# Projection weights kept in DRAM as split halves between two super-blocks

## Chip, core and metric

The kernel runs on one core of a Trainium2 chip. The metric is the device time of one execution in microseconds (us). TensorE is called PE below (its weight loads PEld), VectorE DVE, ScalarE ACT, GpSimd POOL. SP is SyncE, which issues all DMAs of this kernel and runs no arithmetic.

## What is computed

With DEPTH = 1 only layer 0 of the reference runs: a gated DeltaNet layer over 2048 tokens of width 1024, with 8 heads of 128, in float32, and a final norm.

```python
h = x + gated_deltanet_mixer(rms_norm(x, a_norm_w), a_w_in, ...)
out = rms_norm(h, final_norm_w)
# the mixer
proj = h @ w_in                                   # 2048x1024 @ 1024x4112
qkv, z, b_raw, a_raw = split(proj)
q, k, v = split(silu(causal_depthwise_conv(qkv, conv_w)))
o = chunk_gated_delta_rule(l2(q), l2(k), v, beta, g_log)   # state S_t, chunk by chunk
y = rms_norm(o, o_norm_w) * silu(z)
return y @ w_out
```

## The kernel before

**Super-blocks and units.** The 2048 tokens are worked in two super-blocks (`sb` 0 and 1) of 1024. A unit is one head in one super-block, so there are 16 units (`u` 0 to 15; the first 8 belong to super-block 0). Before each super-block `phase0` norms eight tiles of x (128 tokens each), transposes them on PE, and keeps them as two float32r halves `xh` and `xl`; `gates` works out the decays and writes them to DRAM as `gd`, from where `decay` reads them broadcast into the tile E and into qe.

**Projections.** A unit needs four weight tiles of 1024 rows by 128 columns: k, q, v and z (`KI`, `QI`, `VI`, `ZI`). `load_w` reads one into the staging tile `wraw` (eight pieces of 512 bytes on each of 128 partitions), and `split_w` makes two halves of it: ACT rounds it to float32r (`hi`), DVE subtracts that from the raw tile (`lo`). `proj` then makes each product of 512 tokens from 24 matmuls: hi with xh, hi with xl, lo with xh, for eight blocks of rows. A pair of halves is used for two blocks of 512 tokens, that is 48 matmuls. The weights do not depend on the super-block, so each of the 32 tiles is loaded and split twice, once in either super-block.

**Buffers.** `hi` and `lo` (and the halves of y in the output stage) live in six buffers that the profile calls `rnd`; `wraw` lives with x tiles, E, U, A and others in eight buffers called `big`; the smaller tiles are in `half`, and PSUM is `bank`.

**The rest of a unit.** `k_side` forms k·k and q·k products and the tile U, `invert` inverts the triangular matrices (U goes to DRAM and back through `d1`, four small writes and one read, the tile called `d` in the profile), `recur` carries the state S over eight chunks: for each chunk PE, DVE and ACT hand work to each other (rho on DVE, n on ACT, S on DVE), with projections of the next unit in between on PE. After all units the output stage multiplies by `w_out`, adds x, norms and writes.

**Order.** Nothing is issued as written: every operation is recorded by the class `Plan` with a due time `prio` (units of one head; `AT` holds the offsets), and `Plan.schedule` lays them out on the five engines by a list scheduler with a cost for each operation and DMA, and with buffers bound as they come free. The resulting order is fixed, each engine runs its own in order, and all instructions have the line of the issue loop, L357. SP, too, works in order: a DMA that waits for its data holds back the DMAs planned behind it. The due time of a weight load is that of its projection plus `AT["w"]` = -0.14, once the due time is 1 or later.

Of the kernel before, what the change touches and what calls it, by code (L numbers as in the profile page):

```python
# [13 lines left out]
F32 = mybir.dt.float32  # L14
# [8 lines left out]
P = 128  # L23
T = 2048
D = 1024
H = 8
# [9 lines left out]
AT = dict(kq0=-0.25, kq1=-0.09, decay=0.0, k0=0.0, k1=-0.07, inv=-0.36, v=0.0, z=-0.58, vside=-0.67, phase=-0.5,  # L36
          gates=-0.31, w=-0.14)
# [324 lines left out]
def tile_gated_deltanet(ctx: ExitStack, tc: tile.TileContext, x, a_norm_w, w_in, conv_w,  # L362
# [5 lines left out]
    dp = ctx.enter_context(tc.tile_pool(name="dp", bufs=1, space=DRAM))  # L368
# [8 lines left out]
    nc = Plan(tc, cp, pp, bufs, shared)  # L377
# [10 lines left out]
    def st(shape, dtype, tag):  # L388
        return nc.tile(tag, shape, dtype)

    def ps(tag, shape=(P, TB)):
        a = nc.tile(tag, (P, TB), F32, psum=True)[0:shape[0], 0:int(np.prod(shape[1:]))]
        return a.rearrange("p (c k) -> p c k", k=shape[2]) if len(shape) > 2 else a
# [125 lines left out]
    def split_w(raw, hi, lo):  # L519
        nc.scalar.copy(hi, raw)  # L520
        nc.vector.tensor_tensor(out=lo, in0=raw, in1=hi.bitcast(F32), op=ALU.subtract)
# [92 lines left out]

    KI, QI, VI, ZI = 1, 0, 2, 3

    def load_w(ty, h):
        hi = st([P, KT, P], F32R, "whi")
        lo = st([P, KT, P], F32R, "wlo")
        raw = st([P, KT, P], F32, "wraw")  # L620
        c0 = ty * D + h * P
        at = nc.prio
        if at >= 1:
            nc.prio = at + AT["w"]
        nc.sync.dma_start(raw, w_in[:, c0:c0 + P].rearrange("(k p) c -> p k c", p=P))
        split_w(raw, hi, lo)
        nc.prio = at
        return hi, lo

    def proj(w, xh, xl, pj, toks=slice(0, TB)):  # L630
        hi, lo = w
        for k in range(KT):
            nc.tensor.matmul(pj[:, toks], lhsT=hi[:, k, :], rhs=xh[:, k, toks], start=(k == 0), stop=False)
            nc.tensor.matmul(pj[:, toks], lhsT=hi[:, k, :], rhs=xl[:, k, toks], start=False, stop=False)
            nc.tensor.matmul(pj[:, toks], lhsT=lo[:, k, :], rhs=xh[:, k, toks], start=False, stop=(k == KT - 1))

    def conv_block(un, ty, tb, pj):
        h = un["h"]
        raw = st([P, CW - 1 + TB], F32, "raw")
        nc.scalar.copy(raw[:, CW - 1:], pj)  # L640
        nc.gpsimd.tensor_copy(raw[:, 0:CW - 1], halo[:, ty * 8 + h, :])
        if tb < NTB - 1 or un["sb"] < NSB - 1:
            nc.gpsimd.tensor_copy(halo[:, ty * 8 + h, :], raw[:, TB:])
        d = half_tile(un, "qkv"[ty], tb)
        nc.scalar.mul(d, raw[:, 0:TB], cwcol(0, ty, h))
        for tap in range(1, CW):
            nc.vector.scalar_tensor_tensor(out=d, in0=raw[:, tap:tap + TB], scalar=cwcol(tap, ty, h), in1=d,
                                           op0=ALU.mult, op1=ALU.add)
        nc.scalar.activation(d, d, AF.Silu)
# [4 lines left out]
    def half_tile(un, tag, j):  # L654
        a = un[tag, j] = st([P, TB], F32, tag)
        return a
# [7 lines left out]
    def project(un, steps, parts=1):  # L664
        for ty, _ in steps:
            if ty not in un["w"]:
                un["w"][ty] = load_w(ty, un["h"])
        pjs = [ps("pj") for _ in steps]
        for i in range(parts):
            for (ty, tb), pj in zip(steps, pjs):  # L670
                proj(un["w"][ty], un["xh"][tb], un["xl"][tb], pj, slice(i * TB // parts, (i + 1) * TB // parts))
                if i < parts - 1:
                    continue
                if ty == ZI:
                    nc.scalar.activation(half_tile(un, "z", tb), pj, AF.Silu)
                else:
                    conv_block(un, ty, tb, pj)
# [248 lines left out]
    NU = NSB * H  # L926
    nc.prio = -0.97
    w_first = {KI: load_w(KI, 0)}
    nc.prio = -0.94
    w_first[QI] = load_w(QI, 0)  # L930
    nc.prio = -0.9
    xhs, xls, pba = phase0(0)
# [4 lines left out]
    for u in range(NU):  # L937
        un = dict(i=u, sb=u // H, h=u % H, xh=xhs, xl=xls, g=gt, w=w_first if u == 0 else {})
        last = u % H == H - 1
        nc.prio = float(u)  # L940
        if prev is not None:
            recur(prev)
        nc.prio = u + AT["kq0"] if u else -0.72
        project(un, ((KI, 0), (QI, 0)), 2 if u == 0 else 1)
        nc.prio = u + AT["decay"]
        decay(un)
        nc.prio = u + AT["k0"]
        k_side(un, 0)
        nc.prio = u + AT["kq1"]
        project(un, ((KI, 1), (QI, 1)))  # L950
        nc.prio = u + AT["k1"]
        k_side(un, 1)
        nc.prio = u + AT["inv"]
        invert(un)
        if last:
            nc.prio = u + AT["v"]
            project(un, ((VI, 0), (ZI, 0), (VI, 1), (ZI, 1)))
        else:
            nc.prio = u + AT["v"]
            project(un, ((VI, 0), (VI, 1)))  # L960
            nc.prio = u + AT["z"]
            project(un, ((ZI, 0), (ZI, 1)))
# [56 lines left out]
```

## Time and profile before

| what | value |
|---|---|
| median of 3 runs | 1241.1 us (1240.69 to 1241.73) |
| the profiled execution's own time | 1240.98 us |
| its span, first to last instruction | 1239.2 us |
| mean granted PE clock | 0.999 |
| busy: PE, PEld, DVE, ACT, POOL | 99%, 83%, 78%, 49%, 14% |
| DMA moved, mean rate | 118.28 MB, 95 GB/s |

The profile is of one execution. Its span leaves 1.8 us of the execution's time outside. Busy shares are means over the whole span; a busy PE is counted from modelled ends of pipelined matmuls, so the distance from one matmul's start to the next one's is the better measure of its pace. A timeline row gives start, duration, engine, line, operation, what it writes and reads, and how often it is repeated; idle time ahead of it and what ended that stand in brackets.

### The profile page before, as it was taken

How to read it: one execution, taken by the hardware profiler on the slowest of the kernel's cores; microseconds unless marked ns; L12 is line 12 of the kernel's file. 1: busy time of each engine (PE TensorE's matmuls, PEld its weight loads, DVE VectorE, ACT ScalarE, POOL GpSimd, SP SyncE). 2: the span in 40 equal slices, each digit the busy share in tenths (PEclk: the TensorE clock that was granted, in tenths of full speed). 3: DMA queues.
4: the chain of work that ended last, by engine and by line, in shares of the span. 5: the costliest groups of instructions: out<-in, count | busy, mean ns of one | idle time of the engine just before them, and what ended most of it. 6: DMA issues, size and time to landing. Idle time of an engine off the chain costs nothing.

```text
span 1239.2 us, 21069 instructions
## 1 busy us (share of the span) xinstructions
PE 1225.3 (99%) x8049; PEld 1024.5 (83%) x8049; DVE 962.2 (78%) x2228; ACT 607.5 (49%) x1297; POOL 170.5 (14%) x265
## 2 busy tenths in 40 slices
PE   8999999999999999999999999999999999999997
PEld 6788888888888888888888888888888888788886
DVE  6779877877787889797878787878787898955553
ACT  5665455544554565557454545463635564322121
POOL 2011011201111312221010202010101020100100
PEclk9999999999999999999999999999999999999999
DMA  7050423232324131422312122222223225547631
GB/s 229 21 165 1 111 66 81 61 81 60 82 61 117 44 96 46 130 71 79 90 54 84 56 81 61 81 61 81 61 82 111 81 86 179 188 128 248 230 102 68
DMA packets 127481, 118.28 MB, mean 95 GB/s; under 512 B 23986, under 2 KB 106515, under 8 KB 127380
## 3 DMA queue, kind: packets, MB, share of 16 engines
q1 hardware_dynamic: 127380, 116.93, 31.5%
q8 instruction: 63, 1.03, 0.4%
q14 instruction: 38, 0.31, 0.1%
HBM read 97.84 MB, written 19.07 MB: 94 GB/s over the span
## 4 chain that ended last, share of the span: by engine, by line
PE 98%; ACT 1%; DVE 1%; issue 0%; DMA 0%; POOLq 0%; POOL 0%; DVEq 0%; ACTq 0%
PE bank L357 98%; ACT half L357 0%; DVE big L357 0%; ACT rnd L357 0%; DVE half L357 0%; DMA big<-in_a_norm_w_dram 0%; ACT L357 0%; DVE rnd L357 0%; ACT xh L357 0%; ACT big L357 0%; DVE xl L357 0%; POOLq L1015 0%; POOL rs L357 0%; ACT raw L357 0%; DVEq L1015 0%
## 5 line engine op out<-in xcount | busy, mean ns | idle before, releaser
L357 PE MATMUL bank<-xh,rnd 128*128 128x512 f32 (+1 forms) x2624 | 871.8, 402 | 0.7 <-ACT xh L357 0.7
L357 PEld LDWEIGHTS bank<-xh,rnd 128*128 128x128 f32 x2624 | 483.0, 189 | 87.9 <-ACT xh L357 1.3
L357 PE MATMUL bank<-xl,rnd 128*128 128x512 f32 (+1 forms) x1328 | 532.5, 401 | 0.1
L357 PEld LDWEIGHTS bank<-xl,rnd 128*128 128x128 f32 x1328 | 251.3, 189 | 43.2 <-DVE xl L357 0.4
L357 DVE SCALAR_TENSOR_TENSOR half<-raw,vcol,half 128x512 f32<-128x512 f32 x288 | 213.5, 747 | 31.4 <-ACT half L357 27.0
L357 DVE TENSOR_TENSOR rnd<-big,rnd 128x1024 fp32r<-128x1024 f32 x80 | 97.7, 1221 | 47.8 <-ACT rnd L357 42.4
L357 ACT CAST rnd<-big 128x1024 fp32r<-128x1024 f32 x80 | 83.8, 1048 | 99.4 <-PE bank L357 86.3
L357 ACT ACTIVATE n<-bank,nb 128x128 f32<-128x128 f32 x128 | 47.4, 370 | 168.4 <-PE bank L357 168.4
L357 ACT ACTIVATE half<-half 128x512 f32<-128x512 f32 x128 | 80.9, 632 | 93.1 <-DVE half L357 92.1
L357 ACT COPY raw<-bank 128x512 f32<-128x512 f32 x96 | 56.2, 585 | 83.6 <-PE bank L357 83.1
L357 DVE TENSOR_TENSOR half<-X,big 128x6 f32<-128x6 f32 (+15 forms) x256 | 93.7, 366 | 4.4
L357 DVE TENSOR_REDUCE X<-half 128x2 f32<-128x6 f32 (+15 forms) x256 | 92.0, 360 | 4.1
L357 POOL COPY halo<-raw 128x3 f32<-128x3 f32 x72 | 23.4, 325 | 481.7 <-ACT raw L357 473.6
L357 ACT ACTIVATE half<-big 128x512 bf16<-128x512 f32 (+1 forms) x48 | 37.1, 773 | 85.4 <-issue 42.9
L357 ACT ACTIVATE half<-raw,vcol 128x512 f32<-128x512 f32 x96 | 69.4, 724 | 5.0 <-DVE vcol L357 1.4
L357 POOL TENSOR_TENSOR sk<-ssk,phalf 128x4 f32<-128x4 f32 x32 | 40.3, 1261 | 171.6 <-DVE ssk L357 169.8
L357 DVE SCALAR_TENSOR_TENSOR rho<-bank,eg,half 128x128 f32<-128x128 f32 x120 | 41.6, 347 | 27.3 <-PE bank L357 26.9
L357 DVE SCALAR_TENSOR_TENSOR S<-S,dend,bank 128x128 f32<-128x128 f32 x112 | 38.6, 345 | 26.0 <-PE bank L357 25.0
L357 POOL TENSOR_TENSOR rs<-ss,nhalf 128x1 f32<-128x1 f32 x32 | 23.6, 737 | 252.3 <-DVE ss L357 245.0
L357 DVE TENSOR_TENSOR big<-bank,big 128x512 f32<-128x512 f32 x32 | 22.1, 691 | 45.2 <-PE bank L357 45.2
L357 ACT ACT_TABLE_LOAD x42 | 53.9, 1283 | 1.5 <-PEq L1003 0.7
L357 PEld LDWEIGHTS bank<-rho,V 128*128 128x128 f32 x256 | 46.8, 189 | 9.2
(116 smaller groups left out, 1615.1 us busy)
## 6 DMA issues: line engine op xcount, KB each, us to landing
big<-in_a_w_in_dram SPq DMA_DIRECT2D x64, 512.0 KB
big<-in_x_dram SPq DMA_DIRECT2D x32, 512.0 KB
big<-gd SPq DMA_DIRECT2D x16, 512.0 KB
half<-gd SPq DMA_DIRECT2D x32, 256.0 KB
big<-d SPq DMA_DIRECT2D x16, 512.0 KB
yd<-half SPq DMA_DIRECT2D x32, 256.0 KB
big<-yd SPq DMA_DIRECT2D x16, 512.0 KB
big<-rd SPq DMA_DIRECT2D x16, 512.0 KB
```

The lines of the kernel that those rows point to most:

```text
L357: ins = getattr(getattr(self.tc.nc, op[6]), op[7])(*args, **kwargs)
```

## The change

`load_w` gets the super-block as an argument. In super-block 0 it does what it did, and then writes both halves to a DRAM tile `w_d`, two DMAs of 512 KB, with 4 KB in one piece for each partition. In super-block 1 it has no `wraw` and no split: two DMAs read the halves from `w_d` straight into the two buffers that the matmuls use. All DMAs go through SP's queue.

```diff
+    w_d = [dp.tile([H, 2, P, D], F32, name=f"wd{t}") for t in range(4)]
+
-    def load_w(ty, h):
+    def load_w(ty, h, sb=0):
         hi = st([P, KT, P], F32R, "whi")
         lo = st([P, KT, P], F32R, "wlo")
+        if sb:
+            at = nc.prio
+            nc.prio = at + AT["w"]
+            nc.sync.dma_start(hi.bitcast(F32).rearrange("p k c -> p (k c)"), w_d[ty][h, 0])
+            nc.sync.dma_start(lo.bitcast(F32).rearrange("p k c -> p (k c)"), w_d[ty][h, 1])
+            nc.prio = at
+            return hi, lo
         raw = st([P, KT, P], F32, "wraw")
...
         nc.sync.dma_start(raw, w_in[:, c0:c0 + P].rearrange("(k p) c -> p k c", p=P))
         split_w(raw, hi, lo)
+
+        nc.sync.dma_start(w_d[ty][h, 0], hi.bitcast(F32).rearrange("p k c -> p (k c)"))
+        nc.sync.dma_start(w_d[ty][h, 1], lo.bitcast(F32).rearrange("p k c -> p (k c)"))
         nc.prio = at
...
-                un["w"][ty] = load_w(ty, un["h"])
+                un["w"][ty] = load_w(ty, un["h"], un["sb"])
```

## Rows read from the trace of the kernel before

**Rows 1.** The page, busy time: us, share of the span, instructions.

```profile
PE 1225.3 (99%) x8049; PEld 1024.5 (83%) x8049; DVE 962.2 (78%) x2228; ACT 607.5 (49%) x1297; POOL 170.5 (14%) x265
```

**Rows 2.** Stretches: length, busy us (instructions) by engine, clock, DMA share, GB/s.

```profile
core 0: us, PE busy (x) PEld busy (x) DVE busy (x) ACT busy (x) POOL busy (x), PEclk, DMA share, GB/s
0.00:36.00 36.00, 30.15 (x180) 25.56 (x181) 24.37 (x45) 20.69 (x38) 9.39 (x25) 1.00 0.70 212
...
36.00:574.00 538.00, 537.76 (x3649) 449.26 (x3648) 438.29 (x1051) 294.97 (x619) 88.01 (x134) 1.00 0.27 75
583.00:1053.00 470.00, 469.77 (x3243) 395.50 (x3244) 385.85 (x916) 239.44 (x529) 54.01 (x86) 1.00 0.28 82
...
1200.00:1240.00 40.00, 31.86 (x140) 25.86 (x138) 13.99 (x29) 4.86 (x14) 2.20 (x4) 0.95 0.22 79
```

**Rows 3.** The chain that ended last, in order of time: start, length, what.

```profile
36.56 537.79 PE bank L357 x3640
574.37 1.05 ACT rnd L357
...
577.49 1.22 DVE rnd L357
...
583.23 648.65 PE bank L357 x4173
1231.90 0.70 DVE big L357
```

**Rows 4.** Timeline of PE, after a change of kind, and at the boundary.

```profile
66.46 0.48 PE L357 MATMUL bank<-xh,rnd 128*128 128x512 f32 x1
66.78 0.39 PE L357 MATMUL bank<-xl,rnd 128*128 128x512 f32 x1
67.02 0.63 PE L357 MATMUL bank<-xh,rnd 128*128 128x512 f32 x2
67.48 0.39 PE L357 MATMUL bank<-xl,rnd 128*128 128x512 f32 x1
...
583.23 0.49 PE L357 MATMUL bank<-half,half 128*128 128x128 f32 x2 [0.43 <-ACT half L357]
```

**Rows 5.** Groups by operation: busy us, mean ns, idle before and its releasers.

```profile
L357 DVE TENSOR_TENSOR rnd<-big,rnd 128x1024 fp32r<-128x1024 f32 x80 | 97.7, 1221 | 47.8 <-ACT rnd L357 42.4 <-PE bank L357 2.7 <-issue 2.4
L357 ACT CAST rnd<-big 128x1024 fp32r<-128x1024 f32 x80 | 83.8, 1048 | 99.4 <-PE bank L357 86.3 <-DVE big L357 12.1 <-DMA big<-in_a_w_in_dram 0.8
...
L357 PE MATMUL bank<-rho,V 128*128 128x128 f32 x256 | 49.1, 273 | 0.0
```

**Rows 6.** Stretches around one raw load, one write, and one write with a read.

```profile
30.40:34.50 4.10, 4.10 (x24) 3.42 (x23) 3.16 (x5) 2.33 (x6) 0.73 (x2) 1.00 0.48 130
1224.90:1228.00 3.10, 3.10 (x15) 2.59 (x14) 0.74 (x3) 0.72 (x2) 0.00 (x0) 1.00 0.42 169
...
1214.00:1219.00 5.00, 5.00 (x23) 4.13 (x22) 1.48 (x4) 0.72 (x2) 0.00 (x0) 1.00 0.60 210
```

**Rows 7.** Timeline of PE: a buffer's last matmul, and the next weight's first.

```profile
546.84 0.39 PE L357 MATMUL bank<-xl,rnd 128*128 128x512 f32 x1
...
553.52 0.40 PE L357 MATMUL bank<-xh,rnd 128*128 128x512 f32 x1
```

**Rows 8.** Timeline, end of super-block 0: a split on DVE, its first matmuls.

```profile
480.25 1.20 DVE L357 TENSOR_TENSOR rnd<-big,rnd 128x1024 fp32r<-128x1024 f32 x1
...
481.80 0.86 PE L357 MATMUL bank<-xh,rnd 128*128 128x512 f32 x3
```

**Rows 9.** Timeline, start: the last first-phase x tile issued by SP, read by ACT.

```profile
18.66 0.33 SPq L357 DMA_DIRECT2D big<-in_x_dram  x1
...
31.49 1.08 ACT L357 ACTIVATE half<-big 128x1024 bf16<-128x1024 f32 x1
```

**Rows 10.** Timeline, unit 0: tile E issued by SP, first read by DVE.

```profile
61.91 0.34 SPq L357 DMA_DIRECT2D big<-gd  x1
...
68.35 2.16 DVE L357 SCALAR_TENSOR_TENSOR big<-big,g,cst 128x128 f32<-128x128 f32 x8
```

## The prediction

> **What bounds the kernel now.** I read the busy shares first. PE is busy for 1225.3 of the 1239.2 us of the span, DVE for 962.2, ACT for 607.5 [rows 1]. A mean over stages proves little, so next come the stretches. PE's 13.9 idle us sit at the two ends: 36.00 - 30.15 = 5.85 us up to 36 us, and 39.2 - 31.86 = 7.3 us after 1200 us (the last stretch ends 0.8 us past the span). From 36 to 574 us PE is idle for 0.24 us, from 583 to 1053 us for 0.23 us [rows 2]. The chain of waits says the same: one run of PE of 537.79 us, one of 648.65 us, and between them nine microseconds in which the chain goes through ACT and DVE [rows 3]; PE did other work in most of those nine and lost 0.43 us [rows 4].
>
> A busy PE could still be a slow PE, since the ends of matmuls are modelled. The starts settle that: two 512-column matmuls from 67.02 to 67.48 are 0.23 us each, and that pace returns wherever projections follow each other. The first one after another kind is followed at 0.32 us (66.46 to 66.78), so a return from the float32 matmuls of `recur` or `k_side` to a projection costs about 0.09 us [rows 4]. PE is therefore the bound, by its count of matmuls and of such returns, and the change touches neither count directly.
>
> **What is removed.** In super-block 1, 32 casts of ACT and 32 subtractions of DVE: 32 x 1.048 = 33.5 us of ACT and 32 x 1.221 = 39.1 us of DVE [rows 5]. Neither engine is the bound, and in 583 to 1053 us PE waits for them 0.23 us, so this is worth nothing there [rows 2]. It is worth something at one place: the chain between the two PE runs contains one cast of 1.05 us and one subtraction of 1.22 us [rows 3], both of weights of super-block 1 (the raw tiles of units 8 and 9 are loaded ahead). Without them that chain is 2.3 us shorter, more than the 0.43 us that PE loses at its end [rows 4]. I take the whole 0.43 us as gained; the floor is nothing.
>
> Should PE have hidden slack after all, a page would see it. The Trainium skill, Perfetto Trace Analysis, section Identifying the Most-Contended Engine, calls busy matmul time a poor measure of TensorE and wants the busy share of weight loads instead. By that measure PE is 83% busy, 395.50 of 470.00 us in super-block 1, and 39.1 us of removed DVE work could be given back, 1201.9 us. The trace here speaks against reading it as slack: a weight load of 0.19 us inside a pace of 0.23 us shows 81% on an engine that never stops.
>
> **What is added: traffic.** DMA share times length gives the time of all 16 engines. A raw load of 512 KB takes 0.48 x 4.10 = 1.97 us, a write of 512 KB in 4 KB pieces 0.42 x 3.10 = 1.30 us, and one write and one read together 0.60 x 5.00 = 3.00 us, so a read in such pieces 1.70 us [rows 6]. Super-block 0 gets 64 writes, 83 us over 538 us: the share goes from 0.27 to 0.42. Super-block 1 loses 32 raw loads (63 us) and gets 64 reads (109 us), 46 us more over 470 us: from 0.28 to 0.38 [rows 2, 6]. The engines have room. What counts is who waits behind one transfer.
>
> **The reads of super-block 1.** Today a raw tile waits in `big`, and the cast starts when PE has released the buffer (86.3 of ACT's 99.4 idle us ahead of casts end by PE) [rows 5]. Then 2.3 us of split make the pair usable. Afterwards the DMA itself waits for that release, and the pair takes two reads: 3.4 us of transfer and two issues of some 0.4 us, with the landing some 5 us by estimate. I followed each of the six buffers through the order of the matmuls, for the time from a buffer's last matmul to the first one that reads its next weight of super-block 1. From 583 us on that is 13 us at the least and mostly 25 to 40: no cost. The tightest case is the third weight of the super-block, projected ahead near the end of the first, where the x halves' own small weights hold one of the six buffers: released by the matmul at 546.84 us, read by the one at 553.52 us, 6.3 us between [rows 7], against some 4 us for one read with its issue and landing (estimate). PE shouldn't notice; without that cover it pays up to 2 us there, and with none anywhere 32 pairs up to 2.7 us each.
>
> **The writes of super-block 0.** A write must follow its split, and SP, working in order, holds what is planned behind it until then. The matmuls don't wait for a write; the buffer does, but it is held by PE for tens of microseconds longer anyway. At the end of super-block 0 one split ends 0.6 us ahead of its use (480.25 + 1.20, against the third matmul of the row at 481.80) [rows 8]: its raw load must not come later. Raw loads, x tiles, E and the `d` round trip are what can be late. Two places have the least cover:
>
> First the start, 0.70 DMA share up to 36 us [rows 2]. The k and q weights of unit 0 are due ahead of everything, so their four writes go ahead of the last x tiles: 4 x 1.30 = 5.2 us at most. The last x tile is issued at 18.66 and read by ACT at 31.49 us, 12.8 us later [rows 9]; less a load of some 4 us, about 9 us of cover. Cost: nothing; 5.2 us if the cover is gone.
>
> Then unit 0's decays: E is issued at 61.91 and used at 68.35 us, 6.4 us with the load inside [rows 10]; the cover is between nothing and 6.4 - 1.7 = 4.7 us. One pair of writes ahead of it costs 2.6 us, of which PE, with projections queued, pays between nothing and all. I take nothing, as PE's record in that stretch (0.24 us idle in 538) is nearer to it, and keep 2.6 for the range.
>
> **Reordering.** The planner lays out everything anew, with other loads and two engines a little freer. That can shift returns of PE to projections. Eight chunks in 16 units with three stops each (rho has 256 rows, two passes for each of 128 chunks [rows 5]) give about 384 returns, 35 us at 0.09 us. A shift by 5% of them either way is 1.7 us.
>
> **The sum.** 1240.98 (the profiled execution) - 0.43 + 0 + 0 = 1240.55 us. The runs' median lies 0.1 us above that execution, so 1240.7 us. A change under 0.2%, 2.5 us, counts as none.
>
> **Rivals.**
> *Late loads behind the writes (slower).* SP's one queue and the order of writes make E, x tiles or the `d` trip late in super-block 0. For it: E's short cover, and eight units that each have such a trip. Against it: the planner knows of the new DMAs and puts PE work in between. It decides once E or U's way back has less cover than the 2.6 us of a pair. With 2.6 us in unit 0, and 0.5 us in seven more, 6.1 us: 1246.8 us. Chance 0.20.
> *Weights late (slower).* The reads take the place of the split as PE's gate. The 13 us and more, and the 6.3 us of [rows 7], speak against it; it decides if a replanned order leaves under 4 us everywhere. At 2.7 us for each of 32 pairs: 1327 us; chance 0.02.
> *A tidier order (faster).* With ACT and DVE freer, fewer returns in super-block 1: of some 190, a fifth less saves 3.4 us, and the boundary's 0.43: 1237.3 us. For it: DVE is at 82% there. Against: the stops are dictated by the chunks. Chance 0.14.
> *Hidden slack (faster).* PE runs below its pace where DVE is loaded, and gives back up to 39.1 us: 1201.9 us, as the weight-load share would have it. The even pace [rows 4] is against it; 0.02.
>
> The forecast of no change has 0.62, from 1238.6 to 1243.2 us. For the range: 1238.0 leaves out about 0.08 below; 1246.5, the sum and most of the late loads, leaves out 0.11 above. Faster is 0.16, same 0.62, slower 0.22.
>
> **What would show it.** In the profile after: 48 casts and 48 subtractions in place of 80; the chain still two long PE runs, with a shorter piece or none at the boundary; PE idle still some 13.5 us; DMA share about 0.4 in both halves; SP waiting for DVE's and ACT's halves in super-block 0 and for PE in super-block 1. I am wrong if PE shows new idle time in the first 100 us, if rows of PE wait for DMA, or if the count of returns to projections moves by more than a tenth.

## The result, and the profile after

The kernel with the change took 1254.14 us (median, 1253.4 to 1254.72) against 1241.41 us (1240.69 to 1241.79) for the kernel before in the same comparison: a ratio of 1.0102, interval 1.009 to 1.0114. It is 12.7 us slower. The forecast was 1240.7 us, no change, and its range ended at 1246.5.

The profiled execution took 1253.4 us, its span is 1251.6 us. From the page after, the busy times, which answer to [rows 1]:

```profile
PE 1232.1 (98%) x8049; PEld 1026.9 (82%) x8049; DVE 930.9 (74%) x2196; ACT 578.8 (46%) x1265; POOL 164.0 (13%) x265
```

PE has the same 8049 matmuls. It is idle for 1251.6 - 1232.1 = 19.5 us instead of 13.9, and busy for 6.8 us longer with the same work. The groups that answer to [rows 5] show that the change did what it says:

```profile
L357 DVE TENSOR_TENSOR rnd<-big,rnd 128x1024 fp32r<-128x1024 f32 x48 | 58.5, 1221 | 23.3 <-ACT rnd L357 23.1
L357 ACT CAST rnd<-big 128x1024 fp32r<-128x1024 f32 x48 | 50.3, 1048 | 66.0 <-PE bank L357 59.7 <-DVE big L357 6.0
```

There are 48 of each instead of 80, at the same length, so 39 us of DVE and 33 us of ACT are gone. Where the time went is read from the stretches (columns as in [rows 2]):

```profile
0.00:36.00 36.00, 30.06 (x172) 25.61 (x173) 22.33 (x42) 19.50 (x35) 8.80 (x24) 1.00 0.75 241
36.00:50.00 14.00, 10.97 (x49) 8.36 (x48) 11.86 (x22) 9.57 (x15) 1.44 (x3) 0.88 0.16 44
140.00:160.00 20.00, 17.89 (x112) 14.90 (x110) 10.46 (x25) 6.27 (x11) 1.49 (x2) 1.00 0.80 249
160.00:583.00 423.00, 421.87 (x2971) 352.86 (x2970) 347.76 (x841) 224.35 (x482) 70.73 (x109) 1.00 0.42 129
583.00:1053.00 470.00, 470.00 (x3241) 394.72 (x3240) 353.27 (x878) 219.73 (x515) 53.96 (x88) 1.00 0.34 114
```

In the second super-block, from which the work was taken, PE does not stop: it is busy for 470.00 of 470 us. Its new stops are in the first one, most of them at two places: 3.0 us idle and a clock of 0.88 in 36 to 50 us, and 2.1 us idle in 140 to 160 us. The DMA share from 160 to 583 us is 0.42 as forecast, and none of PE's new waits ends by a DMA. The chain of waits says the same: the run of PE that began at 36.56 us and held for 537.79 us [rows 3] now has breaks.

```profile
35.28 0.59 ACT xh L357
35.90 1.29 DVE xl L357 x2
38.49 1.30 DVE big L357
39.93 114.64 PE bank L357 x656
154.56 0.68 DVE half L357
```

The first place on PE's timeline:

```profile
36.22 0.25 PE L357 MATMUL bank<-ident,half 97*128 97x97 f32 x1
37.83 0.43 PE L357 MATMUL bank<-ident,half 32*128 32x32 f32 x4 [1.36 <-DVE ss L357]
39.93 1.81 PE L357 MATMUL bank<-ident,big 128*128 128x128 f32 x8 [1.67 <-DVE big L357]
41.56 1.22 PE L357 MATMUL bank<-xh,rnd 128*128 128x512 f32 x2
42.58 0.63 PE L357 MATMUL bank<-xl,rnd 128*128 128x512 f32 x1
43.01 0.62 PE L357 MATMUL bank<-xh,rnd 128*128 128x512 f32 x1
43.44 0.43 PE L357 MATMUL bank<-xl,rnd 128*128 128x512 f32 x1
```

PE waits twice, for the norm of an x tile (`ss`, then the normed tile in `big`), and after the second wait its projections follow each other at 0.43 us (43.01 to 43.44) instead of 0.23 [rows 4]. A granted clock of 0.88 over 14 us is 0.12 x 14 x 2 = 3.4 us at the half level, 1.2 instead of 2.4 GHz; half of that, 1.7 us, is lost. The x tile that PE waits for is the last one, which [rows 9] follow. SP's queue and ACT, after:

```profile
13.41 1.69 SPq L357 DMA_DIRECT2D wd<-rnd  x2
15.19 0.45 SPq L357 DMA_DIRECT2D big<-in_x_dram  x1
...
19.73 0.33 SPq L357 DMA_DIRECT2D big<-in_x_dram  x1
20.14 0.86 SPq L357 DMA_DIRECT2D wd<-rnd  x2
...
35.28 1.08 ACT L357 CAST xh<-bank 128x512 fp32r<-128x512 f32 x2 [1.89 <-PE bank L357]
36.24 1.07 ACT L357 ACTIVATE half<-big 128x1024 bf16<-128x1024 f32 x1
```

Two of the four writes stand ahead of the last two x tiles. The last tile is issued 1.1 us later than before (19.73 against 18.66) but squared 4.75 us later (36.24 against 31.49), 16.5 us after its issue, and the square stands behind a cast that waited for PE, not for a DMA. So by the trace the tile was there, and its square was called late, by the order of ACT. The second place, PE in the recurrence of unit 0:

```profile
153.51 1.04 PE L357 MATMUL bank<-ident,half 128*128 128x128 f32 x8
155.56 0.49 PE L357 MATMUL bank<-rho,V 128*128 128x128 f32 x2 [1.01 <-DVE rho L357]
156.57 0.49 PE L357 MATMUL bank<-n,half 128*128 128x128 f32 x2 [0.52 <-ACT n L357]
156.89 0.39 PE L357 MATMUL bank<-half,n 128*128 128x128 f32 x2
157.86 0.49 PE L357 MATMUL bank<-S,half 128*128 128x128 f32 x2 [0.58 <-DVE S L357]
...
158.64 0.39 PE L357 MATMUL bank<-xl,rnd 128*128 128x512 f32 x1
158.88 0.40 PE L357 MATMUL bank<-xh,rnd 128*128 128x512 f32 x1
```

Here the stops of a chunk stand one behind the other with no projection between them, so PE sees each handover. The projections behind them are at 0.24 us (158.64 to 158.88), in a stretch with a DMA share of 0.80: the transfers don't slow the matmuls.

**What stops and clock leave over.** The span is 12.4 us longer. PE's idle time makes 5.6 us of that and the half clock 1.7 us; some 5 us are busy time of PE beyond both. Part of this is the pace of the projections. I took the step from one projection's start to the next one's wherever three or more stand in a row; the first step of a row, which [rows 4] put at 0.32 us, and those at the half clock are left out. Over some 2980 steps the mean is 228.6 ns, against 227.7 ns before; that makes 2.8 us. The remaining 2.3 us aren't tied to one place. More returns are not the reason: a projection follows a matmul of another kind 504 times before and 495 times after.

**Two theories.** *Order:* the planner gives each DMA a modelled duration in one modelled queue (`moved` in `schedule`); the counted writes push later arrivals back there, and the order laid out for these imagined arrivals is worse. *Traffic:* the writes and reads themselves delay loads or waiters. Where an expectation speaks of the plan's length, it is the time at which the planner's own model ends, not a measured one.

### The profile page after: what moved, and what is told of

Read it like the earlier page. It is cut to its first block, busy times and chain, and to the rows that moved or that the text cites. A ratio compares the mean times of both kernels' runs of the same rounds, so it can differ in the third digit from the quotient of the medians.

```text
span 1251.6 us, 21148 instructions
## 1 busy us (share of the span) xinstructions
PE 1232.1 (98%) x8049; PEld 1026.9 (82%) x8049; DVE 930.9 (74%) x2196; ACT 578.8 (46%) x1265; POOL 164.0 (13%) x265
## 4 chain that ended last, share of the span: by engine, by line
PE 93%; DVE 4%; DMA 1%; ACT 1%; issue 0%; SPq 0%; POOL 0%; POOLq 0%; DVEq 0%; ACTq 0%
PE bank L357 93%; DVE half L357 2%; DVE X L357 1%; DMA big<-in_a_w_in_dram 1%; DVE big L357 0%; DVE rnd L357 0%; ACT half L357 0%; SPq L357 0%; DVE V L357 0%; DVE T L357 0%; ACT rnd L357 0%; DVE xl L357 0%; DVE rho L357 0%; DMA big<-in_a_norm_w_dram 0%; DVE sumo L357 0%
## 5 line engine op out<-in xcount | busy, mean ns | idle before, releaser
L357 ACT CAST rnd<-big 128x1024 fp32r<-128x1024 f32 x48 | 50.3, 1048 | 66.0 <-PE bank L357 59.7
L357 DVE TENSOR_TENSOR rnd<-big,rnd 128x1024 fp32r<-128x1024 f32 x48 | 58.5, 1221 | 23.3 <-ACT rnd L357 23.1
```

The lines of the kernel that those rows point to most:

```text
L357: ins = getattr(getattr(self.tc.nc, op[6]), op[7])(*args, **kwargs)
```

## Experiments: the writes, counted or issued

**Writes alone.** Super-block 0 as in the change, super-block 1 as before:

```diff
-        if sb:
+        if False:
...
-        nc.sync.dma_start(w_d[ty][h, 0], hi.bitcast(F32).rearrange("p k c -> p (k c)"))
...
+        if not sb:
+            nc.sync.dma_start(w_d[ty][h, 0], hi.bitcast(F32).rearrange("p k c -> p (k c)"))
...
```

> The writes of super-block 0 as in the change; super-block 1 loads and splits its weights as before. The loss of the change (12.7 us) lies in super-block 0 by the traces, so both the order theory (the planner, seeing the writes, lays out a worse fixed order) and the traffic theory (the writes make loads late on SP's queue and the DMA engines) expect about 1252 us, within 3 us. The reads theory (the loss comes with the new reads of super-block 1) expects 1241 us.

Measured: 1251.6 us, ratio 1.0084 (1.0069 to 1.0099). Most of the loss comes with the writes.

**Reads alone.** Super-block 1 reads halves, but only one weight is ever written, by two writes that the planner doesn't see; its halves stand in for all 32, so the output is that of other weights.

> Super-block 1 reads two halves per weight from DRAM, no writes but those of one weight, whose halves stand in for all 32 (so the output is that of other weights); the planner does not see these two writes. Order and traffic theories: 1240 to 1242 us, as nothing is lost in super-block 1. Reads theory: about 1254 us.

Measured: 1246.32 us, ratio 1.0038 (1.0023 to 1.0053). The new order that comes with the reads costs something as well, or the reads do; the runs in the old order below decide that.

**Writes planned, not issued.** The order is that of the run with writes alone, on every engine, and the 64 writes are left out when the plan is issued:

```diff
         for i in self.order:
+            if i in self.skip:
+                continue
...
+            nc.skip |= {len(nc.ops), len(nc.ops) + 1}
```

> The order of e1_writes_only on every engine, but the 64 writes themselves are left out at issue. Order theory: about 1252 us, as with the writes. Traffic theory: about 1241 us, as without the change.

Measured: 1253.1 us, ratio 1.0092 (1.0077 to 1.0107). Its stretches at the two places:

```profile
36.00:50.00 14.00, 11.15 (x43) 8.81 (x44) 10.66 (x17) 8.80 (x13) 1.44 (x3) 0.76 0.01 2
140.00:160.00 20.00, 17.89 (x107) 14.84 (x106) 10.46 (x25) 6.01 (x11) 2.09 (x2) 0.95 0.51 149
```

In 36 to 50 us the DMA engines are all but empty (share 0.01), and PE is idle for 2.85 us with a clock of 0.76 all the same. None of the 64 writes was made, and the loss of the run with writes alone is all there: their traffic isn't its cause.

**Writes issued, not planned.** The mirror image: the plan is made without writes, and each pair goes into SP's queue right behind its subtraction:

```diff
             self.tc.keep_in_program_order(ins)
+            for dst, src in self.behind.get(i, ()):
+                self.tc.keep_in_program_order(self.tc.nc.sync.dma_start(dst, real(src)))
```

> The order of the kernel before on every engine, with each pair of writes put into SP's queue right behind the subtraction that ends its split; super-block 1 as before. Order theory: 1241 to 1243 us. Traffic theory: about 1252 us, or more, since the planner did not make room for them.

Measured: 1243.02 us, ratio 1.0012 (1.0003 to 1.0022). All 64 writes cost 1.5 us in the order of before. That has a place: the load of an x tile for the second super-block stands behind a pair of writes, and ACT, which waited 0.46 us for that tile before, waits 3.37 us; DVE's rho and PE follow. First the row of before, then those of this run:

```profile
457.14 1.06 ACT L357 ACTIVATE half<-big 128x1024 bf16<-128x1024 f32 x1 [0.46 <-DMA big<-in_x_dram]
...
460.07 1.06 ACT L358 ACTIVATE half<-big 128x1024 bf16<-128x1024 f32 x1 [3.37 <-DMA big<-in_x_dram]
...
461.78 0.49 PE L358 MATMUL bank<-rho,V 128*128 128x128 f32 x2 [1.38 <-DVE rho L358]
```

**All transfers, the writes uncounted.** The reads planned as in the change, the writes attached as in the run just told.

> All of the change's transfers are made: the second super-block reads the halves as in the change, and all 64 writes go out, but each pair of them is put into SP's queue right behind its subtraction after the order was laid out, so the planner has not counted them. The order on every engine is that of the run with reads alone (1246.3 us). Order theory (the loss is in the order that is laid out when the writes are counted): 1246.3 plus the 1.5 us that the uncounted writes cost in the old order, 1246 to 1249 us. Traffic theory (writes and reads together load the DMA engines or the HBM): 1252 us or more, as the change itself (1254.1).

Measured: 1247.81 us, ratio 1.005 (1.0035 to 1.0065). That is the run with reads alone plus 1.5 us, as the order theory had it.

## Experiments: the whole change in the old order

**Reads on SP.** The plan of before, casts and subtractions included; at issue the 32 raw loads and splits of super-block 1 are replaced by reads as soon as the buffer's last user is past:

```diff
...
+            if i in self.reread or i in self.skip:
+                for dst, src in reads.get(i, ()):
+                    self.tc.keep_in_program_order(self.tc.nc.sync.dma_start(real(dst), src))
+                continue
...
+            for dst, src in reads.get(i, ()):
+                self.tc.keep_in_program_order(self.tc.nc.sync.dma_start(real(dst), src))
```

> The whole change, in exactly the order of the kernel before on TensorE, VectorE, ScalarE and GpSimd: the plan is made as before with the 32 raw loads, casts and subtractions of the second super-block, and only at issue they are left out; the two reads of halves stand where the last user of their buffers ends, the writes behind their subtractions. Order theory: 1241.4 plus about 1.5 for the writes, less at most 0.5 for the boundary between the super-blocks: 1241 to 1244 us. If the reads themselves cost time (the other reading of the 4.8 us that the run with reads alone lost): 1246 us or more. If freed ScalarE and VectorE time is worth something as soon as the order stays: below 1240.

Measured: 1249.13 us, ratio 1.0067 (1.005 to 1.0083). This was outside what the order theory expected; something in these reads costs. SP, DVE and PE show what:

```profile
651.77 0.40 SPq L372 DMA_DIRECT2D half<-gd  x1
658.94 0.34 SPq L377 DMA_DIRECT2D rnd<-wd  x1
659.46 0.53 SPq L372 DMA_DIRECT2D big<-d  x1
...
661.72 0.70 DVE L372 TRANSPOSE_TENSOR_REDUCE sumo<-half 128x16 f32<-128x512 f32 x1
666.28 0.09 DVE L372 MEMSET big<- 128x32 f32 x1 [3.87 <-DMA big<-d]
...
668.07 0.49 PE L372 MATMUL bank<-S,half 128*128 128x128 f32 x2 [1.84 <-DVE S L372]
```

The read `rnd<-wd` waits at the head of SP's queue for its buffer, some 6.8 us; the way back of the inversion (`big<-d`) stands behind it; DVE waits 3.87 us for that, S comes late, and PE stops for 1.84 us. In all PE waits 5.1 us for S in this run, in five such stops.

**Reads on ScalarE's queue.** The same, with each read issued by ACT in the place of the cast or the subtraction (`nc.scalar.dma_start`), so that SP's queue is free:

> The whole change in exactly the order of the kernel before, as in the run that came out at 1249.1 us, but the two reads of a weight's halves are issued on ScalarE's queue, in the places where the cast and the subtraction stood, so no read waits for its buffer at the head of SP's queue. If that run lost its time because a read that waits for TensorE on SP held up the copies for the inversion behind it (TensorE's gaps of 0.5 to 2.0 us in front of the products with S at 665.8, 731.8, 796.8, 861.0 and 924.7 us): these gaps go and it comes out at 1241 to 1244 us. If the reads cost by their load on the DMA engines, or because freed ScalarE and VectorE time shifts other work: 1246 us or more, with the gaps still there.

Measured: 1243.65 us, ratio 1.002 (1.001 to 1.0029). The same two rows of SP and DVE:

```profile
653.89 0.53 SPq L362 DMA_DIRECT2D big<-d  x1
...
663.25 0.09 DVE L362 MEMSET big<- 128x32 f32 x1
```

`big<-d` goes out at 653.89 instead of 659.46 us, and DVE doesn't wait. PE's waits for S are down to 0.7 us in one stop. So all the transfers of the change, in the order of before and with the reads on ScalarE's queue, cost about 2.5 us (1243.65 against 1241.17). The run with the reads on SP lost 7.5 us; of the 5.0 us between them, 4.4 us are PE's waits for S, one of which the rows follow back to SP's blocked head. Load on the DMA engines isn't the reason, as both runs make the same transfers. The removed 39 us of DVE and 33 us of ACT give nothing that can be seen here.

## Experiments: what the planner counts

**A cheaper DMA in the plan.** The planner prices a 512-byte piece at 60 ns, so a raw load of 1024 pieces on 16 engines at 1024 x 60 / 16 = 3.84 us, where the trace shows 1.97 [rows 6]. One number is changed, in the kernel after and in the kernel before:

```diff
-            each = max(run / (12 if same else 24), 60.0)
+            each = max(run / (12 if same else 24), 31.0)
```

> The change, with one number of the planner's model corrected: a 512-byte piece of a transfer is priced at 31 ns instead of 60 ns, which makes a raw weight load 1.98 us in the plan, as measured (1.97 us of 16 engines), instead of 3.84. All work and all transfers are those of the change. Order theory in its narrower form (the planner holds the x tiles of the start to be late because the writes and the overpriced loads stand before them in its model of the queue): the gaps at 36 to 40 us and the half clock behind them go, 1240 to 1246 us. If counting the writes costs the order something whatever their price, or if it is the traffic: 1250 us or more.

> The kernel before with the same corrected price in the planner, so another order of the same work, and nothing else. It shows what a new order alone does where no write is counted. Order theory: within 4 us of 1241.4, either way (1238 to 1245). The rival that the order of before is a lucky one and every other order loses some 5 to 12 us: 1246 to 1253.

Measured: the change 1245.92 us, ratio 1.0035 (1.0022 to 1.0048), the kernel before 1247.62 us, ratio 1.005 (1.0035 to 1.0065). By this one number the change loses 4.2 us instead of 12.7, and is then 1.7 us faster than the kernel before under the same price. The 4 KB pieces of a write keep their price, so the 64 writes are counted as before, and still the stops at 36 to 40 us and the half clock are gone (a wait of 2.8 us at 13 us is new): it took the counted writes and the overpriced raw loads together to make them. But the kernel before lost 6 us by the new price. That is outside the range of the order theory and inside that of its rival, by which the order of before is a lucky one: an order alone, with not one instruction added, moves the time by this much, and a truer price of one piece does not by itself make a better plan.

**Writes free in the plan.** A write still costs its issue on SP in the plan, but doesn't move the modelled queue:

```diff
-                moved = max(moved, t + dur + 1100) + op[2]
...
+                fast = hasattr(op[8][0], 'tensor') and op[8][0].tensor.name.startswith('wd')
+                if not fast:
+                    moved = max(moved, t + dur + 1100) + op[2]
...
```

> The change with one difference in the planner's model: a write of a half still costs its issue on SP, but it does not push back the later transfers in the modelled queue. All work and all transfers are those of the change. The plan's own length falls from 1226.8 to 1219.8 us and its gaps at 36 to 40 and 150 to 155 us go. Order theory (the modelled transfer time of the writes sets the bad order): 1243 to 1248 us, as other orders of that planned length. If the issue slots of the writes on SP alone, or the traffic, cost the time: 1250 us or more.

Measured: 1246.87 us, ratio 1.0051 (1.0034 to 1.0067), in the range of the order theory: what the writes cost in the plan is their modelled time in the queue. 5.7 us against the kernel before remain.

**Four writes uncounted.** Only the writes of the first two weights are attached after planning; the other 60 are counted as in the change.

> The change, with only the writes of the first two weights (4 of 64) hidden from the planner; they go out right behind their subtractions. The other 60 are counted as in the change. Plan length 1224.9 us; its gaps at 36 to 40 us go, those at 146 to 153 us stay. By the trace of the change the start cost about 5 us, the stretch around 152 about 3: order theory gives 1254.1 less 5, 1248 to 1251 us, with full clock from 36 to 48 us. If the start's loss is from the transfers themselves, or if it was slack that is lost elsewhere: 1253 us or more.

Measured: 1250.09 us, ratio 1.0074 (1.0059 to 1.0089). The two places, first with four writes uncounted, then with all writes free:

```profile
36.00:50.00 14.00, 13.76 (x67) 10.72 (x66) 12.88 (x30) 9.96 (x14) 1.12 (x2) 1.00 0.36 114
140.00:160.00 20.00, 16.79 (x86) 13.77 (x85) 14.25 (x45) 3.86 (x8) 0.00 (x0) 0.91 0.66 210
```

```profile
36.00:50.00 14.00, 13.76 (x67) 10.74 (x66) 12.84 (x30) 9.69 (x14) 1.12 (x2) 1.00 0.35 114
140.00:160.00 20.00, 20.00 (x112) 17.20 (x111) 18.49 (x55) 9.20 (x14) 0.56 (x2) 1.00 0.53 168
```

With four writes uncounted the first place is whole, 13.76 us busy at full clock, though all four are still made. The second is still broken. With no write counted both are whole, though the writes are there.

**A shift that means nothing.** The kernel before with an issue on SP priced at 500 ns in the plan instead of 480; from PE's 653rd instruction on the order differs.

> The kernel before with a shift of the planner's input that means nothing: an issue on SP is priced at 500 ns instead of 480. Same work, same transfers; the plan's length stays (1219.2 us), but from TensorE's 653rd instruction on the order differs. It shows how far the time of one kernel scatters with its order alone. If the order of before is merely a good draw among orders of the same planned length: some us slower, 1243 to 1248, as the run with another transfer price (1247.6). If small shifts do not matter: 1241 to 1242.

Measured: 1241.62 us, ratio 1.0004 (0.9995 to 1.0013). So not every new order is worse, and the rival of the lucky order does not hold for a shift this small. It stays open for larger ones: four runs with another order and no stop at the two places (reads alone, the two with the cheaper piece, writes free) all lost between 4.2 and 6.0 us.

## Why the prediction was wrong, step by step

The runs make a staircase from before to after. The loss is that against the kernel before in the same comparison. The last three columns are read from each profiled execution: PE's idle time (the span less its busy time), time at the half clock (without the last microseconds, where every run has some), and the mean step from one projection to the next, counted as above:

| order and transfers | loss, us | step, us | PE idle, us | half clock, us | mean step, ns |
|---|---|---|---|---|---|
| the kernel before | 0 | | 13.9 | none | 227.7 |
| order of before, all transfers of the change, reads on ScalarE's queue | 2.5 | 2.5 | 14.9 | none | 227.7 |
| order planned with the reads, writes free in the plan | 5.7 | 3.2 | 14.9 | none | 228.9 |
| planned with the reads, 60 of 64 writes counted | 8.9 | 3.2 | 17.7 | 3.4, at 156 us | 228.0 |
| all writes counted: the change | 12.7 | 3.8 | 19.5 | 3.4, at 40 us | 228.6 |

**The step that failed is "Reordering".** It let the planner's new layout shift only returns of PE to projections, 1.7 us either way, and the rival of late loads was priced down because "the planner knows of the new DMAs and puts PE work in between". The opposite holds: the planner's knowledge of the DMAs is most of the loss. 3.2 + 3.2 + 3.8 = 10.2 of the 12.7 us come with the order, and with the writes planned but not made the time is 1253.1 us. The count of returns fell, from 504 to 495. What the term left out are stops of PE, 5.6 us with another 1.7 for the half clock behind them, and a slower pace of the projections, 2.8 us by the mean step. The first of the prediction's own signs of being wrong, new idle time of PE in the first 100 us, is what the profile after shows.

**The pace, "that pace returns wherever projections follow each other".** I took one pair at 0.23 us for the pace of every order. The second and third row of the staircase make the same transfers and have PE idle for the same 14.9 us; the busy time differs, with the same 8049 matmuls (reads on ScalarE's queue, then writes free in the plan):

```profile
PE 1227.0 (99%) x8049; PEld 1024.9 (83%) x8049; DVE 928.7 (75%) x2196; ACT 577.8 (47%) x1265; POOL 171.2 (14%) x265
PE 1229.8 (99%) x8049; PEld 1024.7 (82%) x8049; DVE 933.0 (75%) x2196; ACT 575.0 (46%) x1263; POOL 164.4 (13%) x265
```

A mean step longer by 1.2 ns, over some 2980 steps, is 3.7 us, enough for the whole of this row's 3.2 us. The kernel before under the cheaper price has this slower pace too, 228.9 ns, with no transfer added; every run in the order of before has 227.6 to 227.7.

**The start, "Cost: nothing; 5.2 us if the cover is gone".** The 9 us of cover that I read from [rows 9] were there, and by the trace the x tile came in time. But the order is not made from the trace. In the plan the raw loads in front cost 3.84 us each, and a write by the same formula 128 pieces x 170.7 / 16 = 1.37 us. Two writes ahead of the last x tiles move these tiles by 2.7 us in the plan, their squares go behind other work of ACT, and PE pays. I held the real queue's slack against a modelled queue that has none. What the lost order costs is also more than a shift: PE's two waits are 1.36 + 1.67 = 3.0 us, and the half clock behind them costs 1.7. Together that is more than the last step of the table, 3.8, which is not the start alone: the second place is milder in the change (2.1 us idle at full clock, against 3.2 us and a half clock with four writes uncounted), and the pace of the projections is slower again.

**The traffic** was right: share 0.42 and, with 0.34, a little under the 0.38 forecast for the second super-block. **The price of the writes**, nothing with up to 2.6 us kept, came out at 1.5 us in the order of before, by the very mechanism of the rival (a load late behind a pair of writes), but at an x tile of the second super-block and not at E. **The reads** are hidden in the order of before when nothing waits behind them (2.5 us with the writes against 1.5 for the writes alone, so 1.0 at most), and 4.0 us from issue to landing, the median in the profile after, is the estimate for one read. I had missed what stands behind a read that waits on SP, 5.0 us in the run that put them there in the order of before. In the change itself, where the planner places the reads on SP, PE waits for S only once, 0.6 us.

**The removed work is worth nothing**, as said. The 0.43 us at the boundary [rows 4] do come back: PE's waits in the run with the reads on ScalarE's queue have no wait for ACT's `half` any more. **Hidden slack** is ruled out: there 32 casts and 32 subtractions are gone in an unchanged order, the time rises by 2.5 us, and the mean step stays at 227.7 ns. The Trainium skill, Perfetto Trace Analysis, section Identifying the Most-Contended Engine, judges the room on TensorE by the busy share of weight loads, next to the share of peak FLOPs; by that measure the 83% in this run would be room, and no run here shows any.

**Small slips.** In super-block 1, 395.50 of 470.00 us are 84%; the 83% is the share of the whole span. The band of no change has its lower end, 1238.6, at 2.5 us below the 1241.1 of the kernel before, and its upper end, 1243.2, at 2.5 us above the forecast. The estimate of 384 returns counts those of `recur` alone; with all kinds there are 504. None of them moves the forecast.

**What stays open.** What in a plan sets the pace of the projections: a plan fixes the order and the buffers of all tiles, and no run changes one without the other. It is open, too, whether any larger change of the plan loses some 5 us against the plan of before, whatever it is laid out for. And the steps of the table are differences between whole orders, so each can hide a gain beside its loss, as the fourth row does: more stops, but a better pace than the third.

## What to carry to other kernels

When a static planner lays out the order, ask what its model will make of each new DMA, not only what the DMA engines will: here the added transfers cost 2.5 us on the chip, and the order laid out for them another 10.2. Test it with two runs, one that plans the transfers and leaves them out, and one that makes them in the old order; together they split order from traffic. Compare the pace of the engine that bounds the kernel as well as its stops: a new order can be slower without one more stop. With PE busy to 99%, work taken off other engines bought nothing here, and a DMA that waited for a buffer on SP held up what stood behind it in the queue.

## What the runs showed of the hardware

PE's granted clock fell to the half level after some 3 us of waits within 4 us (1.36 and 1.67 us, from 36.5 to 39.9 us), and stayed there for 3.4 us although PE was busy again. In the run with planned but unissued writes the same two waits were followed by 6.7 us (a clock of 0.76 over 14 us). In the run with four writes uncounted the stops around 150 us do the same: 0.91 over 20 us is 3.6 us at the half level. A single stop of 1.84 us, in the run with the reads on SP, was followed by the pace of before (0.23 us from 668.85 to 669.08) and a clock of 1.00. A stop of PE thus can cost more than its length.

The pace of the projections doesn't follow the DMA load. In the order of before the mean step is 227.7 ns with a DMA share of 0.27 (36 to 574 us, the kernel before) and with 0.43 (the same stretch, all transfers, reads on ScalarE's queue). It does change with the plan: 228.9 ns in the kernel before under the cheaper price, at a share of 0.26.
